# Moving the starts of the matmul operands in SBUF: weights at multiples of 1024 bytes, the other operand 64 bytes behind one

## Chip, core and metric

One core of a Trainium2 chip. The metric is the device time of one execution in microseconds, the median over several runs.

## What is computed

A decoder trunk of two layers over 256 positions of width 1024, batch 1, float32 in and out:

```
layer 0 (even): h = rmsnorm(x);  p = h @ w_in
                y_a = gated spatial mixing of p[:, :1024]   (chunks of 128 positions)
                y_b = RWKV-7 time mixing of p[:, 1024:]     (8 heads of 64, a recurrence)
                x = x + concat(y_a, y_b) @ w_out
layer 1 (odd):  qkv = rmsnorm(x) @ w_qkv
                x = x + dilated window attention(qkv) @ w_out   (16 heads of 64)
each layer:     z = rmsnorm(x) @ w_up           (1024 -> 2 x 2816)
                z = causal convolution of width 3 over positions, plus bias
                x = x + (silu(gate) * val) @ w_down      (2816 -> 1024)
at the end:     rmsnorm(x)
```

## The kernel before, in words

Activations lie with features on the 128 partitions and the 256 positions along a row: the residual stream is `R[128, 8, 256]`. Precision comes from splitting. A float32 operand is written as a high part in the `float32r` type (a ScalarE copy) and a low part, the rest (a VectorE subtraction), and a product is made of three matmuls: high x high, high x low, low x high (`mm3`, all recorded at L174 in `mm`).

Weights come in pieces of up to 128 x 1024 elements through `make_piece`: a DMA on SP's queue into `raw` (4 buffers), then `load` makes `whi` on ScalarE (L243) and `wlo` on VectorE (L244), 4 buffers each. `piece()` keeps two pieces ahead of the one in use. There are 204 pieces.

The stages follow one another on TensorE: projections of the even layer (`layer_even`, in an order on TensorE that a planner in `drive` writes out from costs and waits, with the recurrence's small float32 matmuls in between) and its output projection; the FFN (`ffn`); values, queries and keys, attention and its output projection (`layer_odd`, TensorE's order by hand too); the second FFN with a final product and the last norm (`finish`).

- In most products the weights are the loaded operand (128 columns) and X, H, `yb` or `ya` is streamed (256 columns): `gemm_fm`, the down-projection, the output projections. In `gemm_tm` (values) and in `finish` it is the other way round: X or H is loaded, and the weights are streamed, 256 or 512 columns at a time.
- `ffn` runs 22 iterations over feature tiles. Each takes two pieces (gate and value), 2 x 8 x 3 = 48 matmuls into one of 3 `pg` banks. Then VectorE scales the bank into `z` (L177), ScalarE makes the first tap of the convolution (L960), VectorE adds the other two (L961, L962, for gate and value each), ScalarE takes Silu (L963), GpSimd multiplies gate and value (`y<-y`, L177), ScalarE writes H's high part (`hh`, L284) and VectorE its low part (`hl`, L177). In four iterations of the second FFN, TensorE also transposes tiles of R (`pm`, L970). The down-projection of the first FFN then makes 8 tiles of 22 x 3 = 66 matmuls, and needs all 22 tiles of H for each. `finish` makes 11 pieces x 12 matmuls of 512 columns, then 11 pieces x 24 of 256 columns, the last three of them from `wend`.

Each engine takes its instructions strictly in its own order, which is settled when the program is built.

SBUF tiles come from pools that are laid out one after the other, a tile's row rounded up to 32 bytes: constants (`cpool`), weights (`wpool`), `act` (R and X), small tiles (`sm`), and then one pool per stage that takes the place of the stage before. The start of a tile behind the last multiple of 1024 bytes comes out as follows (a slice of 128 weights is 512 bytes, so every other one begins 512 bytes later; a slice of X or H is 1024 bytes):

```
tile                                          before    after
raw, whi, wlo (weights)                          320        0
R, X (xh, xl)                                    320       64
H (hh, hl), ya (yah, yal)                        960       64
yb (ybh, ybl), warm-up tile idle                   0       64
keys of the attention                            448        0
queries of the attention                         448       64
wend (the last three weight pieces)               32        0
```

Lines that the steps below touch: `mm` L174, `tt` L177, `load` L243 and L244, `split` L284, `ffn` L955 to L970, `finish`.

Of the kernel before, what the change touches and what calls it, by code (L numbers as in the profile page):

```python
# [8 lines left out]
F32 = mybir.dt.float32  # L9
F32R = mybir.dt.float32r  # L10
I32 = mybir.dt.int32
# [148 lines left out]
def body(nc, tc, A, out):  # L160
# [4 lines left out]
    cpool = ctx.enter_context(tc.tile_pool(name="cpool", bufs=1))  # L165
    wpool = ctx.enter_context(tc.tile_pool(name="wpool", bufs=1))
    act = ctx.enter_context(tc.tile_pool(name="act", bufs=1))
    sm = ctx.enter_context(tc.tile_pool(name="sm", bufs=2))
# [8 lines left out]
        (eng or V).tensor_tensor(o, a, b, op)  # L177


    R = act.tile([128, KT, T], F32, name="R")  # L180
    pc = cpool.tile([128, NPA], F32, name="pc")
    warm = cpool.tile([128, 2], F32, name="warm")
# [1 line left out]
    S.dma_start(pc[:, :NPC], A["pcol"][:, :NPC])  # L184
    S.activation(warm[:, 0:1], warm[:, 1:2], AF.Sigmoid)
    cst = cpool.tile([128, _CC["abias"]], F32, name="cst")
    csti = cpool.tile([128, 128], I32, name="csti")

    def C(k, n):
        return cst[:, _CC[k]:_CC[k] + n]  # L190
# [1 line left out]
    def P(k, i=0):  # L192
        return pc[:, _PC[k] + i:_PC[k] + i + 1]
# [2 lines left out]
    omu = cpool.tile([128, 14], F32, name="omu")  # L196
    V.tensor_scalar(omu, pc[:, _PC["mu"]:_PC["mu"] + 14], -1.0, 1.0, op0=OP.mult, op1=OP.add)
    oka = cpool.tile([128, 4], F32, name="oka")
    V.tensor_scalar(oka, pc[:, _PC["k_a"]:_PC["k_a"] + 4], -1.0, 1.0, op0=OP.mult, op1=OP.add)

    DN = ((0, 8), (8, 7), (15, 7))
    AHEAD, LAST = 2, 3
    last = {}
# [42 lines left out]
    def make_piece(src, k, n):  # L246
# [12 lines left out]
        elif made:  # L259

            for i in range(4):
                SP.dma_start(R[:, 2 * i:2 * i + 2], A["xT"][:, 2 * i:2 * i + 2])
                for t in parts:
# [5 lines left out]
                for j in (2 * i, 2 * i + 1):  # L269
                    sq = last["pool"].tile([128, T], F32, name="sq8", tag="t2", bufs=8)  # L270
                    if j in DSQ:
                        tt(sq, R[:, j], R[:, j], OP.mult)
                    else:
                        S.activation(sq, R[:, j], AF.Square)
                    if 0 < j < 6:
# [19 lines left out]
    def norm_hilo(x, gname, k):  # L295
        S.activation(x[0][:, k], R[:, k], AF.Copy, scale=P(gname, k))
        V.scalar_tensor_tensor(x[1][:, k], R[:, k], P(gname, k), x[0][:, k].bitcast(F32), op0=OP.mult, op1=OP.subtract)

    def norm_tile(n, x, gname, k):
        S.activation(x[0][:, k], R[:, k], AF.Copy, scale=P(gname, k))  # L300
        V.scalar_tensor_tensor(x[1][:, k], R[:, k], P(gname, k), x[0][:, k].bitcast(F32), op0=OP.mult, op1=OP.subtract)  # L301
# [10 lines left out]
    def norm_new():  # L312
        return {"acc": sm.tile([128, T], F32, name="sqacc", tag="sqacc", bufs=2)}
# [68 lines left out]
    def layer_even(nxt):  # L382
        pool = tc.tile_pool(name="ev", bufs=1)
        ev = pool.__enter__()
        order = tc.manual_schedule(engines={mybir.EngineType.PE})
        order.__enter__()
        last["pool"] = ev
        n = norm_new()

        def t2(name, dt=F32, tag="t2"):  # L390
            return ev.tile([128, 2, T], dt, name=name, tag=tag, bufs=8 if tag == "t2" else 2)
# [6 lines left out]

        lora = t4("lora")
        L = ev.tile([128, 2, T], F32, name="L")  # L400
        DD = ev.tile([128, 16, 65], F32, name="DD")
        gate, r_, v_ = [ev.tile([128, 4, T], F32, name=x) for x in ("gate", "r_", "v_")]
        WR = ev.tile([128, 2, 16, 192], F32, name="WR")
        BK = ev.tile([128, 16, 192], F32, name="BK")
        SV = ev.tile([128, 2, 4, 4, 64], F32, name="SV")
        blkr = ev.tile([128, 4, 128], F32, name="blkr")
        kx = [t2(f"k{h}", tag="k") for h in range(2)]
        XTs = [None, None]
        YB = [None, None]
        scrA = dr.tile([2, 16, 4160], F32, name="scrA")  # L410
# [26 lines left out]
        def projections():  # L437


            idle = t2("idle", F32R)  # L440
            G.memset(idle.bitcast(F32), 0.0)
            pz = mps()
            for _ in range(WARM):
# [117 lines left out]
        def stream(h):  # L561
# [5 lines left out]
            if h == 0:  # L567
# [5 lines left out]
                for h_ in range(2):  # L573
# [10 lines left out]
                    yield ("pe", 1740, RAT["lora"])  # L584
                G.memset(DD[:, :, 0:1], 1.0)
                when["pre"], WHEN["pre"] = clock[0], cnt[0]
# [4 lines left out]
            for i in range(2):  # L591
                V.tensor_tensor_scan(cum[:, i], C("reset", 256), sig[:, i], 0.0, op0=OP.mult, op1=OP.add)
            S.activation(DD[:, g8, 1:65], chunks(cum), AF.Exp, scale=-DECAY)
            S.activation(DI, cum, AF.Exp, scale=DECAY)
# [19 lines left out]
            for p in range(2):  # L614
                q = slice(64 * p, 64 * p + 64)
                tt(WR[q, p, g8, 0:64], chunks(kk[q]), DD[q, g8, 0:64], OP.mult)
            tt(k_, k_, a, OP.mult)
# [7 lines left out]
            for p in range(2):  # L625
                q = slice(64 * p, 64 * p + 64)
                tt(WR[q, p, g8, 64:128], chunks(r_[q, jsl]), DD[q, g8, 1:65], OP.mult)

# [311 lines left out]
    def ffn(l, n, nxt, gname):  # L940
        pool = tc.tile_pool(name=f"ff{l}", bufs=1)
        fp = pool.__enter__()
        H = [fp.tile([128, FT, T], F32R, name=f"h{x}{l}") for x in "hl"]
        if l == 1:
            Rt = fp.tile([128, 2, D], F32, name="Rt")
            last["pool"] = fp
        for i in range(FT):
            o = gps()
            for y_, _ in enumerate(gemm_fm(o, X)):
                if i == 0 and y_ == 9:  # L950
                    norm_stats(n)
                if i == 0 and y_ == 14:
                    norm_rows(n)
            z = fp.tile([128, 2, T + 2], F32, name="z", tag="z", bufs=3)
            G.memset(z[:, :, 0:2], 0.0)  # L955
            tt(z[:, :, 2:T + 2], o, n["rb2"], OP.mult)
            y = fp.tile([128, 2, T], F32, name="y", tag="y", bufs=3)
            for g in range(2):
                ch = i + FT * g
                S.activation(y[:, g], z[:, g, 2:T + 2], AF.Identity, scale=P(f"cw{l}2", ch), bias=P(f"cb{l}", ch))  # L960
                V.scalar_tensor_tensor(y[:, g], z[:, g, 1:T + 1], P(f"cw{l}1", ch), y[:, g], op0=OP.mult, op1=OP.add)  # L961
                V.scalar_tensor_tensor(y[:, g], z[:, g, 0:T], P(f"cw{l}0", ch), y[:, g], op0=OP.mult, op1=OP.add)  # L962
            S.activation(y[:, 0], y[:, 0], AF.Silu)  # L963
            tt(y[:, 0], y[:, 0], y[:, 1], OP.mult, G)
            split(H[0][:, i], H[1][:, i], y[:, 0])
            if l == 1 and i in (2, 3, 4, 5):
                b, e = i % 2, (i - 2) // 2
                pt = mps()
                for d in range(4):
                    PE.transpose(pt[:, 128 * d:128 * d + 128], R[:, 4 * e + d, 128 * b:128 * b + 128], ident)  # L970
                S.copy(Rt[:, b, 512 * e:512 * e + 512], pt)
        if l == 1:
            finish(H, fp, Rt)
            pool.__exit__(None, None, None)
            return
        for d in range(KT):
            o = gps()
            for k0, kn in DN:
                w = piece()
                for k in range(kn):  # L980
                    mm3(o[:, 0], w, k, slice(0, 128), H, k0 + k, k0 + k == 0, k0 + k == FT - 1)
            out_tile(nxt, gname, d, o[:, 0])
        pool.__exit__(None, None, None)
# [59 lines left out]
    def layer_odd(n, nxt):  # L1043
        pool = tc.tile_pool(name="od", bufs=1)
        od = pool.__enter__()
        vt = od.tile([128, 2, 1024], F32, name="vtok")
        Yt = [od.tile([128, KT, T], F32R, name=f"ya{i}") for i in "hl"]
        ab = od.tile([128, 384], F32, name="abias")
        SP.dma_start(ab, A["cst"][:, _CC["abias"]:])
        blocks = ((0, 128), (128, 384))  # L1050

        keys = [[od.tile([128, 2, T], F32R, name=f"k{x}{i}") for x in "hl"] for i in range(2)]
        for k in keys:
            for x in k:
                G.memset(x.bitcast(F32), 0.0)
        qks, sTs = {}, {}

        def values(c):
            o = gps()
# [128 lines left out]
```

## Time and profile before

| | us |
|---|---|
| median of 3 runs | 693.08 (691.78 to 695.56) |
| the profiled execution, its own time | 690.13 |
| its span, first to last instruction | 688.3 |
| TensorE busy with matmuls | 659.4 |
| VectorE busy | 510.0 |
| ScalarE busy | 395.9 |
| GpSimd busy | 108.8 |

Matmuls are pipelined: each stands in the trace with a duration (280 ns and more for 256 columns) that overlaps the next one's. The pace is the distance from start to start, and a TensorE that is busy all the time may still be pacing slower or faster. Where a row holds several instructions (x463), its time over their count is the pace.

### The profile page before, as it was taken

To read this page: it belongs to the slowest core of one execution; us is meant where nothing else is said; L and a number is where in the kernel's file an instruction comes from. 1 tells how busy PE (TensorE), PEld (TensorE's weight loads), DVE (VectorE), ACT (ScalarE), POOL (GpSimd) and SP (SyncE) were. 2 spreads that over 40 slices of the span, in tenths; PEclk is the share of its full clock that TensorE was granted. 3 is DMA by queue.
4 is the path that set the end of the run, shared out by engine and by line. 5 is a ranking of instruction groups with operands and counts; after the bars stand their busy time and mean duration, and the time that the engine had idled before them with its cause. 6 is when DMAs were issued, how large, how long until landed. Compare 5 with 4: busy or idle time off the path is not lost.

```text
span 688.3 us, 14444 instructions
## 1 busy us (share of the span) xinstructions
PE 659.4 (96%) x5766; PEld 629.1 (91%) x5766; DVE 510.0 (74%) x944; ACT 395.9 (58%) x710; POOL 108.8 (16%) x154
## 2 busy tenths in 40 slices
PE   8999889799999999998999999999999999999996
PEld 7898777689899999998999999998999999998895
DVE  6899966647888888887555469886887888887543
ACT  6766344224776666665444468766576666665431
POOL 4100000200422222221112000001222222221000
PEclk9999999789999999999999999999999999999999
DMA  8656264204455555556665553332754554556531
GB/s 253 237 176 197 72 171 101 63 1 155 136 183 174 182 184 170 172 165 194 179 194 195 176 161 124 123 125 91 245 179 162 182 179 166 179 182 204 193 124 61
DMA packets 44915, 110.33 MB, mean 160 GB/s; under 512 B 16432, under 2 KB 18096, under 8 KB 44848
## 3 DMA queue, kind: packets, MB, share of 16 engines
q1 hardware_dynamic: 31104, 105.03, 47.6%
q10 hardware_dynamic: 13584, 3.86, 2.4%
q8 instruction: 45, 0.74, 0.5%
q0 software_dynamic: 160, 0.52, 0.3%
q14 instruction: 22, 0.18, 0.1%
HBM read 106.50 MB, written 2.90 MB: 159 GB/s over the span
## 4 chain that ended last, share of the span: by engine, by line
PE 69%; DVE 17%; ACT 4%; POOL 4%; DMA 2%; issue 2%; ACTq 1%; SPq 0%; POOLq 0%; DVEq 0%
PE pg L174 54%; PE pm L174 14%; DVE wlo L244 5%; POOL y L177 2%; DVE WR L177 2%; DVE y L961 1%; DVE z L177 1%; DVE xl L301 1%; DMA scrA<-BK 1%; ACT whi L243 1%; PE pm L1108 1%; DVE ftmp L177 1%; ACT y L963 1%; ACT hh L284 1%; DVE y L962 1%
## 5 line engine op out<-in xcount | busy, mean ns | idle before, releaser
L174 PE MATMUL pg<-xh,whi 128*128 128x256 f32 x1008 | 292.7, 290 | 0.7 <-ACT whi L243 0.4
L174 PE MATMUL pg<-xh,wlo 128*128 128x256 f32 x1008 | 286.9, 285 | 1.7 <-DVE wlo L244 1.7
L174 PE MATMUL pg<-xl,whi 128*128 128x256 f32 x1008 | 287.0, 285 | 0.8 <-DVE xl L301 0.7
L244 DVE TENSOR_TENSOR wlo<-raw,whi 128x1024 fp32r<-128x1024 f32 (+2 forms) x199 | 234.2, 1182 | 52.5 <-ACT whi L243 51.4
L243 ACT ACTIVATE whi<-raw 128x1024 fp32r<-128x1024 f32 (+2 forms) x199 | 201.1, 1017 | 88.2 <-PE pg L174 56.4
L174 PEld LDWEIGHTS pg<-xh,whi 128*128 128x128 f32 x1008 | 194.8, 193 | 6.6 <-issue 3.9
L174 PEld LDWEIGHTS pg<-xl,whi 128*128 128x128 f32 x1008 | 194.9, 193 | 2.1 <-DVE xl L301 1.7
L174 PEld LDWEIGHTS pg<-xh,wlo 128*128 128x128 f32 x1008 | 194.6, 193 | 2.4 <-DVE wlo L244 2.3
L177 POOL TENSOR_TENSOR y<-y 128x256 f32<-128x256 f32 x44 | 63.4, 1442 | 30.3 <-ACT y L963 29.9
L284 ACT ACTIVATE hh<-y 128x256 fp32r<-128x256 f32 x44 | 18.3, 417 | 71.0 <-POOL y L177 71.0
L174 PE MATMUL pg<-hh,whi 128*128 128x256 f32 x176 | 49.6, 282 | 2.8 <-ACT hh L284 2.8
L177 DVE TENSOR_TENSOR hl<-y,hh 128x256 fp32r<-128x256 f32 x44 | 18.7, 425 | 45.3 <-ACT hh L284 45.3
L960 ACT ACTIVATE y<-z,pc 128x256 f32<-128x256 f32 x88 | 48.2, 594 | 6.0 <-DVE z L177 0.7
L174 PE MATMUL pg<-hl,whi 128*128 128x256 f32 x176 | 49.6, 282 | 0.1
L174 PE MATMUL pg<-hh,wlo 128*128 128x256 f32 x176 | 49.5, 281 | 0.0
L177 POOL TENSOR_TENSOR sqacc<-sqacc,sq 128x256 f32<-128x256 f32 x21 | 18.7, 892 | 170.3 <-ACT sq L309 169.9
L962 DVE SCALAR_TENSOR_TENSOR y<-z,pc,y 128x256 f32<-128x256 f32 x88 | 38.5, 479 | 0.0
L961 DVE SCALAR_TENSOR_TENSOR y<-z,pc,y 128x256 f32<-128x256 f32 x88 | 38.5, 479 | 0.0
L174 PEld LDWEIGHTS pg<-hh,whi 128*128 128x128 f32 x176 | 33.1, 188 | 3.0 <-ACT hh L284 3.0
L174 PEld LDWEIGHTS pg<-hl,whi 128*128 128x128 f32 x176 | 33.1, 188 | 0.3 <-DVE hl L177 0.3
L174 PEld LDWEIGHTS pg<-hh,wlo 128*128 128x128 f32 x176 | 33.1, 188 | 0.0
L955 POOL MEMSET z<- 128x4 f32 x44 | 4.3, 104 | 168.2 <-ACT y L963 138.9
(247 smaller groups left out, 1049.5 us busy)
## 6 DMA issues: line engine op xcount, KB each, us to landing
raw<-w_up SPq DMA_DIRECT2D x88, 512.0 KB, 3.5
raw<-w_dn SPq DMA_DIRECT2D x30, 512.0 KB, 3.5
raw<-w_qkv SPq DMA_DIRECT2D x24, 512.0 KB, 3.5
raw<-w_in SPq DMA_DIRECT2D x20, 512.0 KB, 4.9
raw<-w_dn SPq DMA_DIRECT2D x16, 448.0 KB, 3.8
raw<-ev_wo SPq DMA_DIRECT2D x8, 512.0 KB, 4.1
raw<-od_wo SPq DMA_DIRECT2D x8, 512.0 KB, 4.0
R<-xT SPq DMA_DIRECT2D x4, 256.0 KB, 3.9
```

Of the source, the lines that this page charges most:

```text
L174: PE.matmul(o, l, r, start=start, stop=stop, skip_group_check=shared)
L177: (eng or V).tensor_tensor(o, a, b, op)
L243: S.activation(hi[:, c], raw[:, c], AF.Copy)
L244: last["lo"] = V.tensor_tensor(lo[:, c], raw[:, c], hi[:, c].bitcast(F32), OP.subtract).ins
L284: S.activation(hi, src, AF.Copy)
L301: V.scalar_tensor_tensor(x[1][:, k], R[:, k], P(gname, k), x[0][:, k].bitcast(F32), op0=OP.mult, op1=OP.subtract)
L955: G.memset(z[:, :, 0:2], 0.0)
L960: S.activation(y[:, g], z[:, g, 2:T + 2], AF.Identity, scale=P(f"cw{l}2", ch), bias=P(f"cb{l}", ch))
L961: V.scalar_tensor_tensor(y[:, g], z[:, g, 1:T + 1], P(f"cw{l}1", ch), y[:, g], op0=OP.mult, op1=OP.add)
L962: V.scalar_tensor_tensor(y[:, g], z[:, g, 0:T], P(f"cw{l}0", ch), y[:, g], op0=OP.mult, op1=OP.add)
L963: S.activation(y[:, 0], y[:, 0], AF.Silu)
L1108: PE.transpose(pt[:, 128 * i:128 * i + 128], sc[:, 128 * i:128 * i + 128], ident)
```

## The change

No instruction of the computation changes. Tiles that nobody uses (`pad_r`, `pad_c`, `pad_s`, `pad_z`, `pad_a`, `pad_q`) are put between the others, the table of integers `csti` moves from the constants' pool to the even layer's, `DD` moves behind the ring of `t2` tiles, and `idle`, the tile that the warm-up matmuls read, is taken from that ring earlier. The starts that result stand in the table above.

```diff
+    act.tile([128, 16], F32, name="pad_r")
     R = act.tile([128, KT, T], F32, name="R")
...
     cst = cpool.tile([128, _CC["abias"]], F32, name="cst")
-    csti = cpool.tile([128, 128], I32, name="csti")
...
     oka = cpool.tile([128, 4], F32, name="oka")
+
+    cpool.tile([128, 48], F32, name="pad_c")
...
         last["pool"] = ev
+        sm.tile([128, 96], F32, name="pad_s", tag="pad_s", bufs=1)
         n = norm_new()
...
         L = ev.tile([128, 2, T], F32, name="L")
-        DD = ev.tile([128, 16, 65], F32, name="DD")
         gate, r_, v_ = [ev.tile([128, 4, T], F32, name=x) for x in ("gate", "r_", "v_")]
...
         kx = [t2(f"k{h}", tag="k") for h in range(2)]
+        last["idle"] = t2("idle", F32R)
+        DD = ev.tile([128, 16, 65], F32, name="DD")
+        csti = ev.tile([128, 128], I32, name="csti")
...
-            idle = t2("idle", F32R)
+            idle = last["idle"]
             G.memset(idle.bitcast(F32), 0.0)
...
             z = fp.tile([128, 2, T + 2], F32, name="z", tag="z", bufs=3)
+            if i == 0:
+                fp.tile([128, 216], F32, name="pad_z")
             G.memset(z[:, :, 0:2], 0.0)
...
         ab = od.tile([128, 384], F32, name="abias")
+        od.tile([128, 112], F32, name="pad_a")
         SP.dma_start(ab, A["cst"][:, _CC["abias"]:])
...
         qks, sTs = {}, {}
+        od.tile([128, 16], F32, name="pad_q")
```

## Rows read from the trace of the kernel before

**Rows 1.** The page, part 1: busy us, share of the span, instructions.
```profile
PE 659.4 (96%) x5766; PEld 629.1 (91%) x5766; DVE 510.0 (74%) x944; ACT 395.9 (58%) x710; POOL 108.8 (16%) x154
```
**Rows 2.** Busy time by stage: stretch, its length, each engine's us, clock, DMA.
```profile
core 0: us, PE busy (x) PEld busy (x) DVE busy (x) ACT busy (x) POOL busy (x), PEclk, DMA share, GB/s
24.00:105.00 81.00, 75.36 (x842) 66.24 (x838) 72.75 (x147) 50.13 (x102) 2.11 (x8) 0.98 0.54 160
316.00:371.30 55.30, 55.30 (x466) 55.30 (x467) 33.73 (x36) 26.38 (x37) 6.08 (x6) 1.00 0.65 194
395.00:474.00 79.00, 79.00 (x638) 74.34 (x638) 59.74 (x186) 52.97 (x133) 0.00 (x0) 1.00 0.39 126
```
**Rows 3.** Timeline of TensorE in the first up-projection: start us, us, instruction; seven starts.
```profile
229.94 0.28 PE L174 MATMUL pg<-xl,whi 128*128 128x256 f32 x1
...
230.66 0.28 PE L174 MATMUL pg<-xl,whi 128*128 128x256 f32 x1
```
**Rows 4.** Timeline of TensorE in the even layer's output projection; seven starts.
```profile
163.93 0.28 PE L174 MATMUL pg<-ybh,whi 128*128 128x256 f32 x1
...
164.61 0.28 PE L174 MATMUL pg<-ybh,whi 128*128 128x256 f32 x1
```
**Rows 5.** The chain that ended last: start us, us, engine, tile, line, count.
```profile
315.99 55.22 PE pg L174 x463
...
378.31 27.71 PE pg L174 x231
...
508.03 0.44 PE pm L970 x4
508.46 5.75 PE pg L174 x48
...
527.04 92.16 PE pg L174 x768
619.19 32.11 PE pm L174 x144
...
677.21 4.33 PE pg L174 x36
```
**Rows 6.** Timeline of VectorE over one up-projection iteration; in brackets, idle before and releaser.
```profile
244.59 0.68 DVE L177 TENSOR_TENSOR z<-pg,rb 128x512 f32<-128x512 f32 x1
245.20 1.23 DVE L244 TENSOR_TENSOR wlo<-raw,whi 128x1024 fp32r<-128x1024 f32 x1
246.34 0.88 DVE L961 SCALAR_TENSOR_TENSOR y<-z,pc,y 128x256 f32<-128x256 f32 x2
247.13 0.88 DVE L962 SCALAR_TENSOR_TENSOR y<-z,pc,y 128x256 f32<-128x256 f32 x2
247.92 1.22 DVE L244 TENSOR_TENSOR wlo<-raw,whi 128x1024 fp32r<-128x1024 f32 x1
250.23 0.43 DVE L177 TENSOR_TENSOR hl<-y,hh 128x256 fp32r<-128x256 f32 x1 [1.08 <-ACT hh L284]
250.57 0.68 DVE L177 TENSOR_TENSOR z<-pg,rb 128x512 f32<-128x512 f32 x1
```
**Rows 7.** Timelines of ScalarE and of GpSimd: that iteration, and the stage's first product.
```profile
249.78 0.42 ACT L284 ACTIVATE hh<-y 128x256 fp32r<-128x256 f32 x1 [1.71 <-POOL y L177]
...
248.28 1.47 POOL L177 TENSOR_TENSOR y<-y 128x256 f32<-128x256 f32 x1
...
189.98 0.75 POOL L177 TENSOR_TENSOR y<-y 128x256 f32<-128x256 f32 x1 [0.95 <-ACT y L963]
```
**Rows 8.** Waits, 185 to 316, and (last row) 497 to 630: total us, times, longest.
```profile
DVE hl L177 <- ACT hh L284: 22.6, 21, 1.1
...
PE pg L174 <- ACT hh L284: 2.8, 1, 2.8
...
DVE z L177 <- PE pg L174: 0.6, 1, 0.6
```
**Rows 9.** Timeline of VectorE at the end of the second up-projection.
```profile
629.83 3.50 DVE L244 TENSOR_TENSOR wlo<-raw,whi 128x1024 fp32r<-128x1024 f32 x3 [0.52 <-ACT whi L243]
```

## Prediction

> **What bounds the kernel now.** I read the page's busy line first, then the stretches by stage, then single matmul starts, then the chain of waits, and last the queues of VectorE, ScalarE and GpSimd in one FFN iteration. TensorE is busy 659.4 of 688.3 us [rows 1], but a busy TensorE can still be starting its matmuls more slowly than it could, so the pace has to be read from start times. Nearly all its work is one form: load 128 columns of weights, stream 256 columns.
>
> The pace differs between stages, with the same shape, the same precision and a clock of 1.00. In the first up-projection seven starts span 229.94 to 230.66: 0.72 / 6 = 120 ns [rows 3]. In the last part of the even layer's output projection they span 163.93 to 164.61: 0.68 / 6 = 113 ns [rows 4]. In the first down-projection it is 55.22 / 463 = 119 ns [rows 5]. What differs is which tiles are read. Adding up the tiles in their order of allocation (each rounded to 32 bytes) puts the weights 320 bytes behind a multiple of 1024, X also at 320, the down-projection's H at 960, and the output projection's `yb` tiles at 0. So where the two operands start matters to the pace: 120 with equal starts, 119 at 640 bytes apart, 113 at 320 apart.
>
> How much lower it could go: the transposes of R, each with its own load of 128 columns, take 0.43 to 0.44 us for four, 109 ns each [rows 5]. Streaming 256 columns at a granted clock of 1.00, 2.4 GHz, takes 256 / 2.4 = 107 by itself.
>
> The second reading decides the sum: in the up-projections TensorE does not set the end although it is busy all the time. VectorE's evacuation `z` starts at 244.59 and again at 250.57, 5.98 us apart [rows 6], while TensorE's 48 matmuls need 48 x 0.120 = 5.76. The loop goes through VectorE's own queue: z, a split of weights, four multiply-adds, a second split at 247.92; then GpSimd's product starts at 248.28 and takes 1.47 (0.75 where no split runs beside it), ScalarE's `hh` at 249.78, and VectorE's `hl` at 250.23, for which VectorE has stood still 1.08 [rows 6, 7]. That standing wait comes 21 times and costs 22.6 us [rows 8]. No `z` waits for TensorE in the first up-projection, and one does, for 0.6 us, in the second [rows 8]. So TensorE only eats up a lead here, and at the end of the first one it waits 2.8 us for the last `hh` [rows 8].
>
> **The change part by part.** No instruction that computes or moves data is added or removed. `csti`'s load keeps its place on SP's queue and its size, and its new place is its own space, so nothing new waits for it: 0. `idle` is taken earlier but is still the first of its ring, ahead of the same memset: 0. The pads are never written: 0. If a moved FFN tile had to wait for an old reader, that would stand at the start of an FFN and cost under 1 us. What changes is starts: weights at 0 (every other k-slice at 512) and X, H, `yb` and the attention output at 64.
>
> What a pair 64 bytes apart costs is not in the trace. Bounds: 107 to 109 ns below, from the streaming and the transposes; above, nothing excludes a loss, so one more of the steps seen (120 - 113 = 7) gives 127. I take **110**: the nearest rows show that unequal starts are never dearer on average than equal ones, and the weight load alone allows 109. The upper end of the likely case is 113, the best pair that the trace shows.
>
> At 110, by stage (times of the profiled execution):
> - Even layer to 185: VectorE is busy 72.75 of 81 us in the middle [rows 2], so little. Its last 98 projection matmuls go from 117 on average to 110: 0.7. Some 50 early ones on the path: 0.5.
> - First up-projection, 185 to 316: 0. TensorE would finish early and wait longer for the last `hh`; the loop's 22 x 5.98 stays.
> - Down-projection, 316 to 371, TensorE busy all 55.30 [rows 2]: 465 x (118.7 - 110) = 4.0.
> - Values and q/k with the first part of the attention's output, 371 to 474, chain on TensorE (231 in 27.71, 120 each [rows 5]): 647 back to back x 9.6 = 6.2. VectorE is busy 59.74 of 79 there [rows 2], so it covers; if the softmax came late for its transposes, part of this would go.
> - 474 to 497: VectorE's additions and splits, 0.
> - Second up-projection, 497 to 619: loop again. Four iterations also hold transposes of R and are TensorE's (5.76 + 0.44 = 6.20 against 5.98): 4 x 0.2 = 0.8. Then a lead is cashed in once. The last matmuls that need a split out of the loop are those of the sixth piece of the final product: its split ends at 629.83 + 1.22 = 631.05 [rows 9], while TensorE comes to it at 619.19 + 5 x 12 x 0.232 = 633.1 (144 in 32.11, of which 132 are 512 wide [rows 5]). TensorE can arrive 2.1 earlier and no more.
> - Final product after that: 72 of 512 columns from 232 to 2 x 110 = 220: 0.9; 260 of 256 columns, 120 to 110 (36 in 4.33 at the end [rows 5]): 2.6. The tail after the last matmul stays.
>
> Sum: 0.7 + 0.5 + 4.0 + 6.2 + 0.8 + 2.1 + 0.9 + 2.6 = 17.8. The profiled execution took 690.13 (span 688.3), 3 below the median of 693.08; taken from the median, 693.1 - 17.8 = **675**. At 113 the same sum is 2.5 + 4.1 + 0.8 + 2.1 + 0.4 + 1.7 + 0.1 = 11.7, so 681; at 109 it is 19.5, so 674. If all the 4,200 back-to-back matmuls of 256 columns counted, 4,200 x 9.7 ns would be 41 us; the difference is the loop.
>
> The Trainium skill ("TensorE: Matmul & The Clock Gate", Back-to-back issue gap) gives N / 2.4 + 2.5 ns between warm matmuls, by which an estimate for 256 columns is 109 and the sum 19.5. The trace's 120 and 113 are above it; no run here shows what lies at it with this form.
>
> **The rivals.**
> *Starts don't matter to TensorE*: 120 and 113 would then come from what else runs at the time. For it: the 113 are only 96 matmuls of one stretch, with little GpSimd work beside them. Against it: 768 matmuls of the second up-projection hold 120 (92.16 us [rows 5]) while VectorE and ScalarE come and go in turns, and the pace changes exactly where the tile changes. Then nothing moves: 693. The Trainium skill ("SBUF — State Buffer", Who interferes with whom) has this rule: TensorE's two read ports are its own and it never waits on another engine; it names no dependence on the start. The trace speaks against reading it as "starts are free".
>
> *The new pair collides more.* All operands now start near the same boundary, one 64-byte step apart, nearer than any unequal pair in the trace. One step more makes 127. The up-projection turns into TensorE's when a matmul costs over 5.98 / 48 = 124.5, and from there it pays too: 48 x 0.127 = 6.09, 44 x 0.11 = 4.8; with 465 x 8 = 3.7, 647 x 7 = 4.5, 260 x 7 and 72 x 14 = 2.8 the sum is +15.8, so 709. With the pair at 64 as bad as the equal one it is 693 again.
>
> *The loop gives way as well*: if VectorE's or GpSimd's work came in another order, so that GpSimd's product didn't stand behind a split (0.75 against 1.47 [rows 7]), an iteration could come down to 48 x 0.110 = 5.28: 44 x 0.7 = 31 instead of the 2.9 of lead and transposes, 693 - 14.9 - 31 = 647. Against it: no edit touches these queues.
>
> *Only one of two roles gains.* In the values and in the final product the weights are streamed and X or H is loaded, so the sign of the distance turns round. Without these, 1.8 (180 x 9.8) + 0.9 + 2.6 are lost: 681; with the gain in these alone, 688.
>
> **How the numbers follow.** The forecast (109 to 113 in both roles, 674 to 681) 0.64; one role, or a pace between 113 and 119 (681 to 690) 0.09; starts don't matter or no better than equal (693) 0.12; worse (about 709) 0.08; the loop gives way, wholly or in part (647 to 670) 0.07. Faster by over 0.5%, about what a measurement of this kernel can tell from no change, is 0.64 + 0.09 + 0.07 = 0.80; same 0.12; slower 0.08. The range from 657 to 690 holds the forecast, the one-role cases and the loop's where it gives way in part: 0.64 + 0.09 + 0.06 = 0.79, near 8 in 10.
>
> **What would show it.** Right: up-projection starts at 109 to 113 until the lead is gone; then TensorE shows gaps before weights `wlo` in both up-projections, which it has nowhere there now; `z` still every 5.98; a longer wait than 2.8 for the last `hh`; the down-projection in 51 us instead of 55. The first up-projection still takes about 131 us. Wrong: starts still at 120 with the tiles at 0 and 64, or above 124.5 with `z` moving to TensorE's pace; or `z` nearer than 5.9, which would make my bound by the loop the error.

## The result and the profile after

The changed kernel takes 684.56 us in the median of four runs (683.63 to 688.29), inside the range given; the kernel before, measured beside it, took 693.80 (691.78 to 695.56, four runs). The ratio is 0.988 (95% interval 0.984 to 0.992). The direction came out as forecast, and so did the loop that holds the first up-projection; the pace did not, and the gain is 9.2 us where the sum gave 17.8.

The page of the changed kernel, part 1, answers to [rows 1]: TensorE is busy 5.6 us less, the other engines as before.

```profile
PE 653.8 (95%) x5766; PEld 621.9 (91%) x5766; DVE 509.6 (74%) x944; ACT 395.3 (58%) x710; POOL 108.9 (16%) x154
```

The pace is in the timeline of TensorE. Here are the first and the last of seven starts, three times, in the changed kernel: X in the first up-projection at two times, and `yb` in the even layer's output projection.

```profile
229.69 0.28 PE L174 MATMUL pg<-xh,whi 128*128 128x256 f32 x1
...
230.37 0.28 PE L174 MATMUL pg<-xh,whi 128*128 128x256 f32 x1
...
279.76 0.28 PE L174 MATMUL pg<-xh,whi 128*128 128x256 f32 x1
...
280.47 0.28 PE L174 MATMUL pg<-xh,whi 128*128 128x256 f32 x1
...
169.68 0.28 PE L174 MATMUL pg<-ybh,whi 128*128 128x256 f32 x1
...
170.39 0.28 PE L174 MATMUL pg<-ybh,whi 128*128 128x256 f32 x1
```

0.68 / 6 = 113 ns, then 0.71 / 6 = 118 ns, with the same tiles at the same addresses and the clock at 1.00. Before, the up-projection had 120 [rows 3]; `yb` had 113 [rows 4] and now has 118, so this part got slower. The first lesson stands in these six lines: 64 bytes apart gives one of two paces, and neither is 110.

This profiled execution was the longest of its four (688.29). The kernel was profiled once more later (685.41 against a median of 685.16; the run "again" below), and that profile is used for the stages. In it X runs at 117.8 through the whole first up-projection: the same kernel had the other pace there in another execution. Its chain that ended last, against [rows 5]:

```profile
284.77 1.48 POOL y L177
290.74 1.48 POOL y L177
...
316.65 56.24 PE pg L174 x463
377.63 1.87 PE pg L174 x15
379.95 26.20 PE pg L174 x231
...
525.74 90.45 PE pg L174 x768
616.20 32.17 PE pm L174 x144
...
672.85 4.09 PE pg L174 x36
```

GpSimd's product `y` stands in the chain every 5.98 us at the end of the first up-projection: the loop is the bound there, as the prediction read it. It was so in the kernel before, whose chain has these rows at the same place:

```profile
284.12 1.48 POOL y L177
290.09 1.48 POOL y L177
```

Of the changed kernel's other rows, 231 matmuls of the values and the first q/k take 26.20 instead of 27.71; 768 of the second up-projection 90.45 instead of 92.16, which is 118 each; the last 36 take 4.09 instead of 4.33, 113 each. The wide part, 32.17 for 144, has not moved.

The waits of the changed kernel's first profile in its first up-projection (185 to 320, the PEld row for `wlo` 185 to 319), against [rows 8]; columns: engine, what waited, for what, total us, times, longest:

```profile
DVE hl L177 <- ACT hh L286: 22.7, 21, 1.1
...
PE pg L174 <- ACT hh L286: 4.7, 1, 4.7
...
PEld pg L174 <- DVE wlo L246: 2.2, 8, 0.4
```

VectorE's standing wait is what it was, and TensorE waits 4.7 us instead of 2.8 for the last `hh` (4.8 in "again"). In this execution, where X ran at 113 for a time, TensorE also waits for weights eight times; in "again", with X at 118, it never does, and in the second up-projection it does so in neither execution. So the sign that the prediction named, gaps before `wlo` in both up-projections, came in one of them and in one execution.

The following table puts both kernels' second profiles (their own times 690.83 and 685.41) side by side, by marks read from the timelines; each row runs from the mark of the row above, and the lead is taken off in the sum:

| stage | before | after | difference | forecast |
|---|---|---|---|---|
| to the last `yb` matmul | 173.18 | 174.94 | +1.8 | -1.2 |
| to the end of the first up-projection's last `hl` | 142.00 | 141.66 | -0.3 | 0 |
| down-projection, to its last matmul | 56.61 | 56.12 | -0.5 | -4.0 |
| values, q/k, attention and its output | 116.77 | 114.50 | -2.3 | -6.2 |
| to the last `z` of the second up-projection | 135.47 | 134.78 | -0.7 | -0.8 |
| lead: final product's first matmul ahead of that `z` | 4.27 | 5.96 | -1.7 | -2.1 |
| final product, 512 columns | 30.67 | 30.80 | +0.1 | -0.9 |
| final product, 256 columns | 31.55 | 29.81 | -1.7 | -2.6 |
| end | 7.06 | 6.96 | -0.1 | 0 |
| sum | 689.05 | 683.61 | -5.4 | -17.8 |

The profiles differ by 5.4, the medians by 9.2, and by 7.7 where "again" was measured (692.89 against 685.16). Beside the later runs the kernel before had medians of 692.9, 692.6, 691.2 and 690.7 (8 to 13 runs each), so its own level moves by 2 us, and both its profiled executions were among its shorter ones. What the profiles show is the 5.4.

### The profile page after: what moved, and what is told of

Read it like the earlier page. It is cut to its first block, busy times and chain, and to the rows that moved or that the text cites. A ratio compares the mean times of both kernels' runs of the same rounds, so it can differ in the third digit from the quotient of the medians.

```text
span 686.5 us, 14444 instructions
## 1 busy us (share of the span) xinstructions
PE 653.8 (95%) x5766; PEld 621.9 (91%) x5766; DVE 509.6 (74%) x944; ACT 395.3 (58%) x710; POOL 108.9 (16%) x154
## 4 chain that ended last, share of the span: by engine, by line
PE 61%; DVE 22%; POOL 6%; ACT 5%; issue 3%; DMA 2%; ACTq 1%; POOLq 0%; DVEq 0%
PE pg L174 45%; PE pm L174 14%; DVE wlo L246 7%; POOL y L177 5%; DVE y L968 2%; DVE z L177 2%; DVE WR L177 2%; DVE xl L303 1%; ACT y L970 1%; ACT hh L286 1%; DVE y L969 1%; DMA scrA<-BK 1%; PE pm L1117 1%; DVE ftmp L177 1%; ACT whi L245 1%
## 5 line engine op out<-in xcount | busy, mean ns | idle before, releaser
L174 PE MATMUL pg<-xh,whi 128*128 128x256 f32 x1008 | 289.4, 287 | 0.9 <-ACT whi L245 0.5
L174 PE MATMUL pg<-xl,whi 128*128 128x256 f32 x1008 | 283.5, 281 | 0.7 <-DVE xl L303 0.6
L174 PEld LDWEIGHTS pg<-xh,whi 128*128 128x128 f32 x1008 | 191.4, 190 | 6.6 <-issue 3.9
L174 PEld LDWEIGHTS pg<-xh,wlo 128*128 128x128 f32 x1008 | 191.3, 190 | 5.0 <-DVE wlo L246 5.0
L174 PEld LDWEIGHTS pg<-xl,whi 128*128 128x128 f32 x1008 | 191.9, 190 | 1.9 <-DVE xl L303 1.3
```

The lines of the kernel that those rows point to most:

```text
L174: PE.matmul(o, l, r, start=start, stop=stop, skip_group_check=shared)
```

## The experiments

**A sweep of the distance.** A kernel in which TensorE alone works: blocks of 48 matmuls of the kernel's form, the streamed operand d bytes behind the loaded one, d from 0 to 992 in steps of 32; block a with weights at 0, b with weights 320 bytes on, c behind a small float32 matmul.

```diff
+        def block(tag, base, d):
...
+            for r in range(2):
+                for k in range(8):
...
+                    wh, wl = w[:, b:b + 128], w[:, 2048 + b:2176 + b]
+                    xh, xl = x[:, 0, m:m + 256], x[:, 1, m:m + 256]
+                    PE.matmul(o, wh, xh, start=True, stop=True)
+                    PE.matmul(o, wh, xl, start=True, stop=True)
+                    PE.matmul(o, wl, xh, start=True, stop=True)
```

> This kernel computes nothing of the reference: it only issues blocks of 48 f32r matmuls (128 columns of weights loaded, 256 columns streamed) from two constant tiles, with the streamed operand 0 to 992 bytes behind the loaded one in steps of 32, the loaded one at 0 or at 320 behind a multiple of 1024. Theory (starts set the pace): block by block the pace differs by distance; 120 ns at distance 0, 113 where a block is free of collisions, nothing below 113 if the cycle of load and stream itself takes 113; at distance 64 either 113 or 118, as both stand in the changed kernel's trace. Rival (starts don't matter, other engines' traffic does): no other engine works here, so all blocks run at one pace, 113 or less. A second question: if only the distance counts, the blocks with the loaded operand at 0 and at 320 agree distance by distance; if the place counts too, they don't.

Measured, from start to start once a block has settled (the very first block apart, 145.6): 120.0 at 0, 117.8 at 32 (116.7 in block c) and at 64, 120 at 96, 118.7 at 128 and 160, 117.8 at 192, 118.3 at 224, and then the same again every 256 bytes, with the weights at 0 or at 320. One block of the 96, c at 960, which is 192 modulo 256, ran at 113.3, and its neighbour at 928 at 117.3. So it is the distance modulo 256 that counts, no other engine is needed for it, and 64 was worth 2 ns in all its blocks, not 10. Nothing came below 113.

**The changed kernel again, the change without its first pad, the kernel before again.** "equal0" leaves the order and every instruction as in the changed kernel, but R, X, H, `yb` and `ya` lie at 0 like the weights:

```diff
-    act.tile([128, 16], F32, name="pad_r")
```

> The changed kernel once more, for a second trace and its time beside the other runs. Theory (the up-projections are held by the loop of VectorE, GpSimd and ScalarE, and the pace of the rest is 113 or 118 by turns): about 684, with z every 5.98 us in both FFNs. If the long half-clock stretch behind the first up-projection (317 to 324 us) belongs to the change, it is here again; if it was that execution's alone, the down-projection takes about 55 us without it.

> The change without the pad ahead of R: weights at 0 and X, H, yb and ya at 0 too, so equal starts as before the change but at a multiple of 1024. Theory (only the distance between the starts counts): 120 ns everywhere as before the change, time about 693, as before. Rival (that the weights begin at a multiple of 1024 is what helps): a pace of 113 to 118 with equal starts, and about 684.

> The kernel before, once more, for a second trace of it. Theory: pace 120 with X, 119 with H, 113 with yb, z every 5.98, the wait for the last hh 2.8 us; what differs from the first trace is where the half-clock stretches lie, and so the span.

"again" took 685.16 (four runs; ratio 0.988, 0.983 to 0.994), "equal0" 691.56 (ten runs; 0.997, 0.994 to 0.999) with X, H and `ya` at 120 ns. Taking away 64 bytes takes away 6.4 of the 7.7 us: the starts are the cause. About the rest stands in its final product, which takes 29.95 and 31.10 us for its two parts instead of 30.67 and 31.55. The chain of waits of "equal0" has two rows of the kernel before [rows 5], 27.71 and 92.16:

```profile
380.33 27.71 PE pg L174 x231
...
530.53 92.16 PE pg L174 x768
```

"before_again" took 690.83 (one run) and is as expected: 120 ns with X, 118.7 with H, 113.5 with `yb`, `z` every 5.98 us, 2.9 us for the last `hh`.

**The loop relieved.** To see what the starts are worth where the loop does not hold the up-projection, GpSimd's product goes to VectorE, in both kernels. The same values are computed.

```diff
-            tt(y[:, 0], y[:, 0], y[:, 1], OP.mult, G)
+            tt(y[:, 0], y[:, 0], y[:, 1], OP.mult)
```

> The kernel before, with the product of gate and value in both FFNs moved from GpSimd to VectorE; starts as before. Theory (the loop over GpSimd's product, which stands behind a split of weights, holds the up-projections at 5.98): without it TensorE sets the pace, z every 48 x 0.120 = 5.76, some 44 x 0.21 = 9 us less less the lead that was already there, about 685. Rival (TensorE held the up-projections already): z at 5.98 or more, since VectorE has more to do, and 693 or slower.

> The same edit on the changed kernel. Theory (TensorE holds the up-projections once the loop is gone, so the starts pay there too): z every 48 x 0.1178 = 5.65, or 5.44 where the pace is 113, and about 671 to 677, that is 8 us or more below the same edit on the kernel before. Rival (VectorE holds them now: two splits, z, four multiply-adds, hl and the product are about 5.2 us): z every 5.2 to 5.5 whatever the starts, and both edited kernels alike.

With the old starts 687.57 (six runs; 0.992, 0.989 to 0.995), where about 685 was expected, with the new ones 679.29 (four runs; 0.979, 0.974 to 0.984), where 671 to 677 was. The old starts' chain shows TensorE without a break through the up-projection and the down-projection, 1,532 matmuls at 183.15 / 1532 = 120 ns, and `z` 5.76 us apart, 48 x 0.120:

```profile
185.41 183.15 PE pg L174 x1532
```

Its waits of VectorE (185 to 316) are for TensorE now, and those with the new starts (185 to 312) for ScalarE's part of the weight split, at 5.72 us per iteration, which neither the theory (5.65 or 5.44) nor the rival (up to 5.5) had:

```profile
DVE z L177 <- PE pg L174: 4.8, 17, 0.3
...
DVE hl L177 <- ACT hh L284: 1.0, 2, 0.5
```

```profile
DVE wlo L246 <- ACT whi L245: 9.6, 20, 0.5
...
DVE hl L177 <- ACT hh L286: 1.0, 2, 0.5
```

VectorE's 22 us for `hh` have gone to 1.0: they were the price of GpSimd's product standing behind a split, and the loop was the bound of the first up-projection in the kernel before as in the changed one. Once it is relieved, TensorE bounds there with the old starts and VectorE with ScalarE with the new ones.

The second up-projection is another matter. From the last matmul of the attention's output to the first of the final product, the kernel before takes 131.20 us and with the product moved 131.21; with the new starts it is 128.81 and 129.02. The loop's relief gains nothing there, because TensorE goes on into the final product without waiting for it: the last `z` may come later, and only TensorE's pace and the cap on its lead count. The chain with the new starts and the product on VectorE runs through TensorE there:

```profile
520.00 90.45 PE pg L174 x768
610.45 32.17 PE pm L174 x144
```

**The other sign.** "off192" puts the weights 64 bytes behind X and H, which makes 192 modulo 256 for a streamed X, and 64 for streamed weights:

```diff
-    act.tile([128, 16], F32, name="pad_r")
+    act.tile([128, 48], F32, name="pad_r")
...
-    cpool.tile([128, 48], F32, name="pad_c")
```

> The changed kernel with the distance turned round: weights 64 behind a multiple of 256 bytes, X, H, yb and ya at one, so that the streamed operand is 192 (instead of 64) behind the loaded one, modulo 256, where weights are loaded, and 64 (instead of 192) where they are streamed. Theory (at distance 192 the cycle locks at 113, as with yb before and in the final product after): 113 with X, H, yb and ya; 118 in the values and the final product; about 683. Rival (64 and 192 are alike, and 113 or 118 is a matter of how a run of matmuls begins): 118 mostly, everywhere, about 685. If the start at a multiple of 1024 counted: 120, 693.

686.14 (four runs; 0.990, 0.985 to 0.994): no different from the change, and 3 us above the 683 of the first theory. H streams at 113.8 in the mean, as that theory has it, and the values and the final product's 256-column matmuls, at 113 to 114 with the change, take 117.8. But X runs at 114.0 in the first up-projection and at 117.8 in the second, at the same distance of 192, and the last pieces of the final product (`wend`), whose distance the edit leaves at 192, go from 113 to 118. So neither theory holds as it stands: 192 too has two paces. Its chain: 54.91 / 464 = 118 for the down-projection, whose first 4 us lie in a stretch of half clock, and 4.25 for the last 36 where the change has 4.09.

```profile
314.37 54.91 PE pg L174 x464
...
672.60 4.25 PE pg L174 x36
```

**A finer sweep.** The same blocks in steps of 8 bytes, d from 0 to 248: f one after the other, h behind a wait for VectorE, j behind a float32 matmul.

> It leaves out the whole computation of the reference: TensorE alone runs blocks of 48 matmuls (load 128 columns, stream 256), the streamed operand 0, 8, 16 ... 248 bytes behind the loaded one modulo 256. Blocks f follow each other without a gap, each block h begins after TensorE has waited for a VectorE copy, each block j behind a small float32 matmul. Theory (113.3 ns is the floor of this form, and a distance only decides how often a stretch settles there): no block goes below 113; distances 0 and 96 stay at 120 whatever goes ahead; the ones at 32, 64 and 192 come out at 117.8 or at 113.3, and which of the two changes with what goes ahead of the block. Rival (the forecast's 110 was to be had, the 64 bytes are only the wrong distance): between the distances tried so far, at steps of 8 and 16 bytes, some block runs at 109 to 111 under all three beginnings. Second rival (the pace is a smooth function of the distance and the beginning has nothing to do with it): f, h and j agree within 0.5 ns at every distance.

The timeline of its TensorE, the 13th and the last of the 48 matmuls (35 starts apart) of the blocks f and j at distance 64, then at 112:

```profile
60.50 0.28 PE L183 MATMUL fSixFour<-x,w 128*128 128x256 f32 x1
...
64.47 0.28 PE L185 MATMUL fSixFour<-x,w 128*128 128x256 f32 x1
...
545.70 0.28 PE L183 MATMUL jSixFour<-x,w 128*128 128x256 f32 x1
...
549.82 0.28 PE L185 MATMUL jSixFour<-x,w 128*128 128x256 f32 x1
...
94.80 0.28 PE L183 MATMUL fOneOneTwo<-x,w 128*128 128x256 f32 x1
...
98.76 0.28 PE L185 MATMUL fOneOneTwo<-x,w 128*128 128x256 f32 x1
...
509.99 0.28 PE L183 MATMUL jOneOneTwo<-x,w 128*128 128x256 f32 x1
...
513.96 0.28 PE L185 MATMUL jOneOneTwo<-x,w 128*128 128x256 f32 x1
```

At 64: 3.97 / 35 = 113.4 behind the block at 56 without a gap, 4.12 / 35 = 117.7 behind the small matmul (117.8 also behind the wait). At 192 the same pair of numbers. At 112: 3.96 and 3.97, which is 113 both times, and 113.3 behind the wait. So the rival that 110 was to be had at another distance falls (nothing is below 113.3), the one of a smooth function falls too (72 bytes gives 121.3, 8 more than 64 at its best), and 64 and 192 have two paces, which change with the work ahead. Smaller pairs of that kind stand at 8 (117.6 and 120.0), 16 (116.7 and 118.7) and 80 (118.3 and 120.1). 112 has only the better one in these three blocks.

**Other sign and product on VectorE.**

> The product on VectorE together with the weights 192 bytes ahead of X and H instead of 64 behind. Theory (the two edits lie in different stages: VectorE sets the up-projections at 5.70 us per iteration, the pace sets the down-projection and the final product): z every 5.70 us again, the down-projection 2 to 3 us shorter than with 64 (H at 113.8 instead of 117.2 per matmul, 465 of them: 1.6 to 1.9), the values and the final product 1 to 3 us longer, in sum 678 to 681, the same as with 64 (679.3). Rival (TensorE's pace of X still sets the up-projections there): at 116.0 instead of 116.1 nothing moves, but where X keeps 113.3 an iteration falls to 5.5 and the time to 670 to 675.

Its four runs took 672.65, 678.04, 683.67 and 683.81; the two shorter ones alone are too few and too far apart to be told from 679.29. `z` came every 5.72 us, as the first theory has it. The shortest had a mean granted clock of 0.987, the others 0.969 to 0.970. In the profile (of 678.04) X runs at 113.4 in both up-projections, where "off192", with the same starts, had 117.8 in the second.

**112 instead of 64.** X, the first FFN's H and `ya` become slices of slightly larger tiles, 112 bytes behind the weights; all else stays where the change put it.

```diff
+    def pair(pool, k, name):
+        t = [pool.tile([128, k * T + e], F32R, name=name + i) for i, e in zip("hl", (16, 64))]
+        return [x[:, e:e + k * T].rearrange("p (k n) -> p k n", k=k) for x, e in zip(t, (12, 60))]
...
-    X = [act.tile([128, KT, T], F32R, name=f"x{i}") for i in "hl"]
+    X = pair(act, KT, "x")
...
-        sm.tile([128, 96], F32, name="pad_s", tag="pad_s", bufs=1)
+        sm.tile([128, 16], F32, name="pad_s", tag="pad_s", bufs=1)
...
```

> The changed kernel with X, the first FFN's H and the attention's output 112 bytes behind the weights modulo 256 instead of 64; the second FFN's H and `yb` stay at 64, instructions and order are the same. Theory (the step that failed is the pace: 64 settles at 117.8 most of the time, 112 at 113.3 whatever goes ahead): X streamed 113 to 114 ns in the mean and with at least 0.8 of its matmuls below 116, H 113.3, ya 113.3, the down-projection 465 x 4.5 = 2.1 us shorter, q/k and the attention's output 1.5 to 2.5 shorter together; the values, where X is the loaded operand and the distance is 144, 0.9 longer (192 x 4.5); the up-projections unchanged at 5.98 us per iteration, with a longer wait for the last `hh`; in sum 3 to 5 us off 684.6, so 679.5 to 682. Rival (112 is good only where no other engine works): H and ya at 117 to 118 and the time 684 to 686. Second rival (nothing below 117.8 pays, since the chains outside TensorE have taken over): H at 113.3 and the time still 684 to 686.

> The same starts together with the product on VectorE. Theory: an up-projection iteration stays at 5.70 us, since VectorE's own work sets it there and 48 x 0.1133 = 5.44 is below it; the down-projection, q/k and the attention's output give the same 3 to 5 us as without the product's move, so 674.5 to 677. Rival (TensorE's pace of 116.1 is what holds an iteration at 5.70, 48 x 0.1161 = 5.57 and its starts): an iteration falls to 5.45 to 5.55, and 44 of them give 7 to 11 us more, 664 to 669.

The pace did what the sweep said: X 114.2 in the mean with 0.85 of its matmuls below 116 (117.5 and 0.07 in the second profile of the change), H 113.6, `ya` 114.5, and streamed weights with X loaded, now at 144, 120.0 instead of 114.8. The 120.0 is 1.3 above what the finer sweep has at 144: the sweeps measured only the other role. The time did not follow: 686.30 (six runs, 684.00 to 688.95; 0.994, 0.992 to 0.996), where 679.5 to 682 was expected. Its profiled execution was the shortest of the six, 684.00, only 1.4 below the profile of "again". In it the down-projection takes 54.3 us instead of 56.1 and the attention's output 27.9 instead of 28.5, as they should, and the 231 matmuls of the values and first q/k 27.21 instead of 26.20. The rest goes in two places. TensorE's windows around the start of the second up-projection:

```profile
484.00:490.00 6.00, 4.43 (x34) 3.83 (x33) 5.58 (x9) 2.58 (x5) 1.58 (x5) 1.00 0.77 273
490.00:493.40 3.40, 3.40 (x18) 3.40 (x17) 1.33 (x3) 1.06 (x1) 0.71 (x1) 0.50 0.77 276
```

TensorE was busy 4.43 of 6.00 us (4.84 of 6.00 at that place in "again"), and behind that the granted clock is 0.50, the level of 1.2 GHz, for 3.4 us, in which it starts 18 matmuls; at 113 ns they need 2.0, so 1.4 us are lost. That this comes from the pace of 112 is not shown: "equal0", at 120, and "off192" have a stretch of 3.4 us at this place too. The second place is the end of the chain of waits:

```profile
622.74 0.80 DVE y L972 x2
623.53 0.41 DVE y L973
623.97 0.43 ACT y L974
624.51 1.56 POOL y L177
626.42 1.05 ACT whi L249
627.50 1.24 DVE wlo L250
628.77 18.20 PE pm L174 x83
```

The final product now stands and waits for the split out of the loop that ends at 628.74, so the lead is spent: the first matmul of the final product came 7.4 us ahead of the last `z`, and its 512-column part took 32.0 instead of 30.8. Of the 1.5 by which the lead is longer than in "again", 1.2 are given back. The second rival of this run (the chains outside TensorE have taken over) holds from the second up-projection on; up to the attention's output the profile is 2.9 us ahead of "again". The other five runs are up to 5 us longer than the profiled one, and their mean granted clock is lower, 0.975 to 0.977 against 0.982. By an estimate, twice the difference times the span (a stretch at 0.50 lowers the mean by half its share), that is 7 to 10 us more at half clock; where these stretches lie, no profile shows.

With the product on VectorE the same starts give 675.69 (four runs, 675.49 to 675.80; 0.978, 0.976 to 0.979), inside the 674.5 to 677 expected; of all kernels' runs only the 672.65 above is shorter. It is 3.6 below the version with 64, but the kernel before measured beside it was 1.9 lower too, and the two ratios, 0.978 and 0.979, are not told apart. The loop's period does not follow TensorE. VectorE's timeline over one iteration, and three rows of the chain:

```profile
241.16 0.69 DVE L177 TENSOR_TENSOR z<-pg,rb 128x512 f32<-128x512 f32 x1
241.76 0.42 DVE L177 TENSOR_TENSOR hl<-y,hh 128x256 fp32r<-128x256 f32 x1
242.68 1.23 DVE L250 TENSOR_TENSOR wlo<-raw,whi 128x1024 fp32r<-128x1024 f32 x1 [0.51 <-ACT whi L249]
...
246.54 0.42 DVE L177 TENSOR_TENSOR y<-y 128x256 f32<-128x256 f32 x1
246.88 0.68 DVE L177 TENSOR_TENSOR z<-pg,rb 128x512 f32<-128x512 f32 x1
```

```profile
309.88 55.37 PE pg L174 x464
...
519.16 87.08 PE pg L174 x768
606.24 32.17 PE pm L174 x144
```

From `z` to `z` 5.72 us, in which VectorE is idle only the 0.51 for `whi` and the product, once 1.48 on GpSimd, takes 0.42. In the first up-projection TensorE therefore ends early and waits. In the second it does not: 768 take 87.08 instead of 90.45, 113 each, and the final product follows without a gap, so there the pace counts in full. That is where most of the difference to the version with 64 lies. Of the 4.2 us between the profiles, 2.3 come between the attention's output and the final product (in spite of a half-clock stretch that the other has not) and 1.4 in the down-projection; the values, q/k and the attention's output together give 0.2. So the time came out as expected partly by luck: the expectation had 3 to 5 us from the down-projection, q/k and the attention's output, and nothing from the second up-projection.

## Why the prediction was right in direction and too large in size

**The step that failed** is "What a pair 64 bytes apart costs is not in the trace", where the prediction took 110. The floor was taken from the transposes of R, 109 ns [rows 5]; in neither sweep nor in any stage of a kernel did the mean of this form go below 113.3. And the distance of 64 was taken for one value, where it has two: 117.8 in most of the stages where the weights are loaded, and 113.3 to 114.8 where they are streamed (192, by the turned sign). The row that was thought to be the best pair, `yb` at 113 [rows 4], was 192 modulo 256 at its better pace, and with the change it went to 118.

With the measured paces in its own sum the prediction comes out (paces of the second profiles): down-projection 465 x (118.7 - 117.8) = 0.4 for 4.0; the values 180 x (119.8 - 113.8) = 1.1 and q/k with `ya` 467 x (119.6 - 117.8) = 0.8, together 1.9 for 6.2; the four iterations with transposes 4 x (6.20 - 5.65 - 0.44) = 0.4 for 0.8; the lead 1.7; 512 columns nothing; the 256-column part 260 x 6.6 ns = 1.7 for 2.6; `yb` -0.4. That makes 5.7. The profiles have 7.2 in the rows behind the first, and 5.4 with the first row's +1.8, which goes with stretches at half clock (below). So most of what lies between 17.8 and the measurement is this one term.

**The rest, step by step.** *First up-projection 0, held by the loop:* right; `z` every 5.98 in both kernels, TensorE's wait for the last `hh` from 2.8 to 4.7, and the runs with the product on VectorE show that the 22 us of standing wait were that loop. *Second up-projection, "loop again":* right only in part. The loop sets `z` there, but TensorE sets the end, as the 131.20 and 131.21 with and without the loop show. *The lead:* right in place and nearly in size, 1.7 for 2.1, since it is TensorE's gain there up to a cap. In the first profile of the change TensorE begins the final product at 618.94, 60 x 0.233 later it is at 632.9, and VectorE's split for the sixth piece ends at 631.43 + 1.2 = 632.6 [rows 9]:

```profile
631.43 4.64 DVE L246 TENSOR_TENSOR wlo<-raw,whi 128x1024 fp32r<-128x1024 f32 x4 [0.53 <-ACT whi L245]
```

With 112 it arrives earlier and waits: 7.43 of lead less the 1.17 that the 512-column part is longer is 2.0 more than the 4.27 of the kernel before, as the cap of 2.1 says. *512 columns 232 to 220:* wrong; 233 with the change, and 227 in "equal0", so the wide form was fastest with equal starts. *Even layer -1.2:* not seen; the last `yb` matmul starts at 173 to 177 in the profiles of all kernels, in no order with the starts. The half-clock stretches ahead of it differ: 13.7 us in all in the second profile of the kernel before (173.2), 17.1 in "again" (174.9), 23.9 in the first profile of the change (177.0); that they are the cause is not shown.

**The rivals.** "Starts don't matter" falls with the sweep. The Trainium skill's rule behind it ("SBUF — State Buffer", Who interferes with whom: only the port pair shared by VectorE and GpSimd makes engines wait) isn't touched: in the sweep no other engine works, and the starts alone move the pace between 113 and 122. "The new pair collides more" falls for 64, though 72 would have given 121. "Only one of two roles gains" was the nearest: the streamed weights gain in full, the loaded ones 2 ns of 7; it was priced at 688 for a gain in the streamed ones alone. What came had a chance of 0.09 there: "one role, or a pace between 113 and 119 (681 to 690)". The Trainium skill's formula ("TensorE: Matmul & The Clock Gate", Back-to-back issue gap), 109 for 256 columns as an estimate, is given there for a matmul apart from its load. No run here shows 109; for loads and matmuls in turn the lowest mean is 113.3.

## What to carry to other kernels

Before moving an operand, measure the pace of the very form (load, stream, type) at the distance in question with TensorE alone, and under more than one beginning: a distance may have two paces. Then ask stage by stage who sets the end, and not from the busy share: of the two up-projections, with nearly the same instructions, the loop through three other engines set the end of the first and TensorE that of the second, where the work behind it can start on the first tiles of H. In the first a faster TensorE gained 0.3 us. In the second it gained up to the first split that it needs out of the loop, and with the loop relieved in full. For 64 bytes the relief of the loop made no clear difference (7.7 and 9.2 us by the medians beside the old loop, 8.3 without it). 112 bytes gave 1.4 us more than 64 in the profiles and nothing in the median beside the old loop, and 4.2 more in the profiles without it; by the ratios to the kernel before this second gain is not told apart from none.

## What the runs showed of the hardware

- A matmul of 256 columns behind a load of 128, both `float32r`, goes at 113.3 to 122 ns at a clock of 1.00, by the distance of the two operands' starts modulo 256 bytes: 120 at 0, 113.3 at 112, 121.3 at 72, up to 122.2 at 120 and 136, and most others between 117 and 120. Where the pair lies makes no difference (weights at 0 or 320).
- At 64 and 192 the pace is 113.3 or 117.8, and it is kept from one matmul to the next until a wait or another pair of tiles comes between. In the first profile of the changed kernel X runs at 113.3 in the first up-projection up to 260.4 us and at 117.8 from 261.1 on, behind the first wait for `wlo`; in "again" it runs at 117.8 there throughout. What in the work ahead picks the pace stays open.
- At the start of the first down-projection, behind 4.7 us in which TensorE waited for `hh`, the granted clock fell to the level of 1.2 GHz. The windows of the first profile of the change show it:

```profile
317.00:324.00 7.00, 5.99 (x27) 5.82 (x28) 3.47 (x5) 3.02 (x5) 0.51 (x1) 0.52 0.64 172
324.00:331.00 7.00, 7.00 (x61) 7.00 (x61) 3.30 (x4) 3.67 (x5) 0.00 (x0) 0.99 0.49 138
```

27 matmuls in 5.99 us against 61 in 7.00: 5.99 - 27 x 0.115 = 2.9 us lost, part of why this execution was the longest of its four. In the profiles of "again", of "equal0" and in the second one of the kernel before, the stretch at this place is 3.4 us long; in the first one of before there is none. How much of it is due to the longer wait these runs don't settle.

- The mean granted clock of a run was 0.986 in the median of 40 runs of the kernel before, 0.980 in 9 of the changed kernel, 0.9765 in 6 of "d112" and 0.977 in 4 with the product on VectorE as well. By the same estimate as above, the 0.006 between the first two is 8 us more at half clock, so a part of what a faster pace gains may be lost this way; that the pace is the cause is not shown.
